# Taking all arithmetic off GpSimd in a two-layer hybrid decoder step

## The chip, the cores and the metric

One core of one Trainium2 chip runs the whole program. The metric is the device time of one execution in microseconds. Engines are TensorE (PE, with its weight loads as PEld), VectorE (DVE), ScalarE (ACT), GpSimd (POOL) and SyncE (SP), whose queue issues nearly all the DMAs.

## The reference

288 tokens (256 of one prompt and 8 samples of 4) pass through two layers. In each layer the normalised residual stream feeds one input projection whose columns go to three token mixers and three gates:

- gated DeltaNet: short convolution on q, k and v, then a chunked form with a triangular solve and a state S;
- retention: rotary q and k, fixed decay per head, a state R;
- mLSTM: exponential gates, a state C and a normaliser n.

```
R = R * c_dec + einsum(k_c * k_dec, v_c)               # retention
S = S * exp(g_last) + einsum(k_c * ..., v_new)         # DeltaNet
Cm = s_dec * Cm + einsum(kw, v_c)                      # mLSTM
x1 * cos - x2 * sin, x1 * sin + x2 * cos               # rotary
```

Each mixer's output is normalised, gated, projected, merged by the gates and projected out; then come a layer norm, a feed-forward part (1024 to 4096 to 1024, squared ReLU) and a layer norm. The updated states of prompt and samples are outputs too.

## The kernel before

Activations lie transposed: features on the 128 partitions, the 288 tokens along the free axis. A weight block (128x1024 fp32, 512 KB) is loaded by SP, split by ScalarE (`wh`, L358) and VectorE (`wl`, L360) into a high and a low part, and multiplied in three passes (`mm3`, L364): 24 matmuls of 288 columns for each 128 outputs. Inside the mixers these projection matmuls also serve as filling (L504) between the small dependent matmuls. Tile's scheduler sets the order on each engine by priority (order in the program) and readiness; at run time every engine takes its instructions in that order. SP too is in order, its DMAs included. Tiles of one kind share a pool: `B` (5040 bytes for each partition) has 18 buffers, and a tile waits for a free one.

In order of the program, for each layer:

- L586 `conv_group`, three times: GpSimd copies the sample's old rows (L591) and the new conv state (L600, L601); ScalarE and VectorE do the convolution.
- L622 to L762: gates, decays and cumulative sums in small VectorE operations on few rows; `dec` (L724) and the transposes behind it need them.
- L572 `rotary`, for rq and rk: two DMAs swap the halves into `rot`, VectorE multiplies by cos (L576), GpSimd by sin (L577), VectorE adds (L578).
- L764 to L797: keys are transposed and copied to KR (L768), squared and summed (`sumsq`, L412), and `rsqrt` (L379) runs eleven small VectorE operations. GpSimd later scales KR by the decay into KP (L858).
- L839 to L847: GpSimd scales the decay matrix E1 by beta (L839), VectorE multiplies it with the key products (L846) into MM. MM goes out to DRAM and returns by blocks (L862 to L867), 15 steps on VectorE invert the diagonal blocks (L869 to L874), the result returns as qc, and GpSimd spreads it into QL (L1056) and masks MM into E32 and E128 (L1062, L1064) for the solve.
- `qmask` (L880): GpSimd multiplies 32 sample columns of four heads with a 0/1 table into 128x1024, so that one matmul (`cross`, L893) picks a sample's rows. It is called for retention (L1017), DeltaNet (L1122, twice) and mLSTM (L1147).
- `vexp` (L925): two GpSimd multiplications with a 0/1 column (L929), three times a layer.
- `finish` (L957): sum of squares (L965), a chain of small VectorE operations (L967 to L974, with `rsqrt`), a scaling (L975), then transposes on PE (L982) and gating (L990, L992).
- `update` (L932): each of four groups of eight states of 128x128. For retention the decay is a constant and the evacuation of the product does all (L948). For DeltaNet and mLSTM GpSimd first multiplies the states by the decays (L937, 128x1024), then VectorE adds the product from PSUM in two halves (L952). The updates wait in a list, `later`, and `tick` runs one behind each tile of the next projection, the gate tiles `pg` of L1252 among them.

Of the kernel before, what the change touches and what calls it, by code (L numbers as in the profile page):

```python
# [58 lines left out]
for _n, _s in (("rm", T), ("mrst", T), ("sgn", 1), ("dsel", 64), ("kdec", 9), ("qdec", 1), ("stk", 10), ("ohbh", 32),  # L59
               ("gsel", 44),  # L60
               ("cos", T), ("sin", T), ("rdiag", 512), ("roff", 512), ("rsam", 128), ("ohr", 256), ("m32", 128),
               ("m128", 128), ("cm16", 128)):
    CONST[_n] = (_W, _s)
    _W += _s
# [3 lines left out]
def host_consts():  # L68
    c = np.zeros((P, CONST_W), np.float32)

    def put(n, a):
        o, s = CONST[n]
        c[:, o:o + s] = a
# [24 lines left out]
    put("rsam", np.where(le, np.exp((tt[None, :] - tt[:, None]) * lg[hh][:, None] * le), 0.0) * ks)  # L98
    put("ohr", np.broadcast_to((np.arange(NB)[:, None] == (np.arange(32) // NS)[None, :]).reshape(1, -1), (P, 256)))
    put("ohbh", ((bb[:, None] == np.arange(NB)[None, :])[:, :, None]  # L100
# [153 lines left out]
def tile_trunk(ctx, tc, a):  # L254
# [4 lines left out]
    def pool(name, bufs, **k):  # L259
        return ctx.enter_context(tc.tile_pool(name=name, bufs=bufs, **k))  # L260
# [3 lines left out]
    xp = pool("xp", 1)  # L264
    bp = pool("bp", 18)
    rp = pool("rp", 9)
# [41 lines left out]
    ones = cp.tile([P, P], F32, name="ones")  # L308
    V.memset(ones, 1.0 / 128.0)
    RB = cp.tile([P, T], F32R, name="RB")  # L310
    V.memset(RB.bitcast(F32), 0.0)
# [91 lines left out]
    def transpose9(src_p, src_s, evac):  # L403

        for g, (u0, u1) in enumerate(GRP):
# [4 lines left out]
            evac(u0, u1, ps[:, :(u1 - u0) * P].rearrange("p (u s) -> p u s", s=P))  # L410

    def sumsq(dst, src9):  # L412

        sq = u9(B("sq"))
        S.activation(sq, src9, AF.Square)
        V.tensor_reduce(dst, sq, axis=AX.X, op=ALU.add)

# [45 lines left out]
    for l in range(L):  # L463
# [108 lines left out]
        def rotary(X_):  # L572
            Y_ = h4(B("rot"))
            SP.dma_start(Y_[0:64], X_[64:128])
            SP.dma_start(Y_[64:128], X_[0:64])
            V.tensor_tensor(X_, X_, bcm(C("cos"), 4), op=ALU.mult)  # L576
            G.tensor_tensor(Y_, Y_, bcm(C("sin"), 4), op=ALU.mult)  # L577
            V.tensor_tensor(X_, X_, Y_, op=ALU.add)  # L578
            return X_
# [6 lines left out]
        def conv_group(gi, seg, st=None, done=()):  # L586
            CV = B("CV")
            cv = CV[:, :4 * CVW].rearrange("p (h w) -> p h w", w=CVW)
            cvs = cv[:, :, SB0:SB0 + 56].rearrange("p h (b w) -> p h b w", w=7)
            G.memset(cv[:, :, 0:3], 0.0)  # L590
            G.tensor_copy(cvs[:, :, :, 0:3],  # L591
                          cstate[:, 96 * gi:96 * gi + 96].rearrange("p (h b w) -> p h b w", h=4, b=NB))

            def ev(j, ps):
                S.copy(cv[:, j, 3:SB0], ps[:, :TP])
                S.copy(cvs[:, j, :, 3:7], ps[:, TP:T].rearrange("p (b t) -> p b t", t=NS))  # L596
            proj(seg, ev, st, done)

            ncv = K("ncv", 4, 27)
            G.tensor_copy(ncv[:, :, 0:3], cv[:, :, SB0 - 3:SB0])  # L600
            G.tensor_copy(ncv[:, :, 3:27].rearrange("p h (b w) -> p h b w", w=3), cvs[:, :, :, 4:7])  # L601
            G.dma_start(a["o_conv"][l, :, 108 * gi:108 * gi + 108], ncv.rearrange("p h w -> p (h w)"))
            CO = B("CO")
            co = CO[:, :4 * CVW].rearrange("p (h w) -> p h w", w=CVW)
            n = CVW - 3
            G.memset(co[:, :, n:CVW], 0.0)
            for j in range(4):
                S.activation(co[:, j, :n], cv[:, j, 0:n], AF.Copy, scale=VEC(l, "conv", gi * 4 + j))
                for w in range(1, 4):
# [156 lines left out]
        co, cs_ = conv["dk"]  # L766
        KR = u9(B("KR"))
        transpose9(lambda c, h: co[:, h, c * P:(c + 1) * P], cs_, lambda u0, u1, ps: S.copy(KR[:, u0:u1], ps))  # L768
        sumsq(ssqk[:, 1], KR)
        rqk = K("rqk", 2, 9)  # L770
# [67 lines left out]
        S.activation(E1[:, 8], ps, AF.Exp, bias=gcol[:, 8:9], scale=-1.0)  # L838
        G.tensor_tensor(E1, E1, bc(br2, P), op=ALU.mult)  # L839
        MM = E1  # L840
        for u0, u1 in GRP:
            ps = PX("G")
            for u in range(u0, u1):
                PE.matmul(ps[:, (u - u0) * P:(u - u0 + 1) * P], kt(u), kt(u), start=True, stop=True)
            fill(FILL_M[1])
            V.tensor_tensor(MM[:, u0:u1], E1[:, u0:u1], ps[:, :(u1 - u0) * P].rearrange("p (u s) -> p u s", s=P),  # L846
                            op=ALU.mult)  # L847

# [7 lines left out]
        PT = E2  # L856
        KP = KR
        G.tensor_tensor(KP, KR, bc(egl, P), op=ALU.mult)  # L858

# [19 lines left out]

        def qmask(qs_ap):  # L880
            m_ = B("qm")[:, :1024].rearrange("p (h b t) -> p h b t", h=H, b=NB)
            q4 = qs_ap.rearrange("p (h t) -> p h t", h=H)
            G.tensor_tensor(m_, q4.unsqueeze(2).to_broadcast([P, H, NB, 32]),
                            C("ohr").rearrange("p (b t) -> p b t", b=NB).unsqueeze(1).to_broadcast([P, H, NB, 32]),
                            op=ALU.mult)
            return m_
# [6 lines left out]
        def cross(ps, qm, st, q, w=P):  # L893
            for i in range(8):
                b, h = 2 * q + i // 4, i % 4
                PE.matmul(ps[32 * h:32 * h + 32, :w], qm[:, h, b, :], st[:, i, :],
                          start=b == 0, stop=b == NB - 1, tile_position=(0, 32 * h))
# [27 lines left out]
        def vexp(src, w):  # L925
            v_ = stack(src, 1, w).rearrange("p (h v) -> p h v", h=H)
            m_ = B("vx", F32R)[:, :1024].rearrange("p (h b v) -> p h b v", h=H, b=2)
            for b_ in range(2):
                G.tensor_scalar(m_[:, :, b_, :], v_.bitcast(F32), C("stk")[:, 4 + b_:5 + b_], None, op0=ALU.mult)  # L929
            return m_  # L930

        def update(st, q, kx, vx, dec, out):  # L932

            st = st[:, :, :P]
            pre = not isinstance(dec, list)
            if pre:
                G.tensor_tensor(st, st, bc(dec[:, 8 * q:8 * q + 8], P), op=ALU.mult)  # L937
            s4 = st.rearrange("p (b h) v -> p b h v", h=H)
            for hh in range(2):
# [6 lines left out]
                for h in (2 * hh, 2 * hh + 1):  # L946
                    if not pre:
                        V.scalar_tensor_tensor(s4[:, :, h, :], s4[:, :, h, :], dec[h], pv[:, :, h % 2, :],  # L948
                                               op0=ALU.mult, op1=ALU.add)
                if pre:  # L950
                    hs = s4[:, :, 2 * hh:2 * hh + 2, :]
                    V.tensor_tensor(hs, hs, pv, op=ALU.add)  # L952
            SP.dma_start(out[l, q].rearrange("p (i v) -> p i v", v=P), st)
# [62 lines left out]
        transpose9(lambda c, h: rv[:, h, c * P:(c + 1) * P], rvs, lambda u0, u1, ps: S.copy(RV[:, u0:u1], ps))  # L1016
        qm = qmask(rqs)  # L1017
        vx, kx = vexp(rvs, C("stk")[:, 6:10]), kexp(rks)
# [18 lines left out]
        for q in range(4):  # L1037
# [17 lines left out]
        QL = u9(B("QL"))  # L1055
        G.tensor_tensor(QL.rearrange("p u (k j) -> p u k j", j=16), qc.unsqueeze(2).to_broadcast([P, 9, 8, 16]),  # L1056
                        C("cm16").rearrange("p (k j) -> p k j", j=16).unsqueeze(1).to_broadcast([P, 9, 8, 16]),
# [3 lines left out]
        E32 = B("E32")[:, :1024].rearrange("p (u s) -> p u s", s=P)  # L1061
        G.tensor_tensor(E32, MM[:, :8], bcm(C("m32"), 8), op=ALU.mult)  # L1062
        E128 = MM
        G.tensor_tensor(E128[:, :8], MM[:, :8], bcm(C("m128"), 8), op=ALU.mult)  # L1064

# [55 lines left out]
        fin_dp = finish(OT, rqk[:, 0], zg, VEC(l, "dnn", 0), 0, 0, 8)  # L1121
        km, qm = qmask(cs_), qmask(cs_q)  # L1122
        kx = kexp(cs_)
# [22 lines left out]
        transpose9(lambda c, h: mv[:, h, c * P:(c + 1) * P], mvs, lambda u0, u1, ps: S.copy(MV[:, u0:u1, :P], ps))  # L1146
        qm_m = qmask(mqs)  # L1147
        vx_m, kx_m = vexp(mvs, WX[:, 1]), kexp(mks)
# [353 lines left out]
```

## Time and profile before

| | |
|---|---|
| median of 3 runs | 1285.8 us (1285.58 to 1287.79) |
| the profiled execution | 1285.11 us |
| its span, first to last instruction | 1283.3 us |
| busy: PE, PEld, DVE, ACT, POOL | 94%, 91%, 71%, 47%, 10% of the span |
| mean granted clock of TensorE | 0.971 |

The span holds both layers: the mixers of layer 0 run to about 285 us, its gates, output and feed-forward part to about 640 us, and layer 1 repeats this from there. The shares are means over these parts; what a wait costs is read in its own part.

### The profile page before, as it was taken

Reading aid. Unit: us, or ns where it says so; the run is one execution under the profiler, and the core shown is the slowest. Engines: PE = TensorE matmul, PEld = TensorE weight load, DVE = VectorE, ACT = ScalarE, POOL = GpSimd, SP = SyncE. Lnnn points to the kernel's source line nnn. Section 1 sums busy time; section 2 is a strip of 40 time slices with the busy share of each in tenths; the row PEclk is TensorE's granted clock in tenths of the full one; section 3 lists DMA queues with packets and bytes.
Section 4 is the critical chain, followed back from the end, with each engine's and each line's share of the span. In section 5 each row is a group of like instructions: output and inputs, shape, how many; then the busy total and the mean of one; then the engine's idle time right before and its main releaser. Section 6 shows DMA issues by size and latency. Waiting matters only on the chain.

```text
span 1283.3 us, 22945 instructions
## 1 busy us (share of the span) xinstructions
PE 1201.7 (94%) x9210; PEld 1169.4 (91%) x9210; DVE 909.0 (71%) x1617; ACT 597.1 (47%) x1006; POOL 126.6 (10%) x107
## 2 busy tenths in 40 slices
PE   9989899889999999999997988998899998999995
PEld 8978799789999899999996987997799998999995
DVE  6988846596558974566899877556856688645665
ACT  5645324433445653455584532453334566534532
POOL 1113400330000000000000413004200000000000
PEclk9989999889999999999998998998899998999998
DMA  8443624348554465555714454253575543655551
GB/s 311 124 146 107 214 85 152 124 181 243 166 167 123 142 181 164 168 168 162 245 57 133 119 176 154 90 182 140 169 211 164 165 156 94 193 166 165 164 165 38
DMA packets 69794, 201.27 MB, mean 157 GB/s; under 512 B 11688, under 2 KB 22232, under 8 KB 69560
## 3 DMA queue, kind: packets, MB, share of 16 engines
q1 hardware_dynamic: 68744, 197.64, 49.1%
q0 software_dynamic: 944, 2.17, 0.5%
q8 instruction: 72, 1.18, 0.4%
q14 instruction: 34, 0.28, 0.1%
HBM read 180.62 MB, written 17.03 MB: 154 GB/s over the span
## 4 chain that ended last, share of the span: by engine, by line
PE 71%; DVE 18%; DMA 4%; ACT 3%; issue 3%; SPq 1%; DVEq 0%; ACTq 0%
PE f L369 9%; PE f L367 9%; PE f L368 9%; PE pj L504 6%; DVE wl L360 5%; PE pg L367 4%; PE pg L368 4%; PE pg L369 4%; PE pj L369 2%; PE pj L368 2%; PE pj L367 2%; PE br L367 2%; PE br L368 2%; PE br L369 2%; DMA wr<-in_w_ff 1%
## 5 line engine op out<-in xcount | busy, mean ns | idle before, releaser
L360 DVE TENSOR_TENSOR wl<-wr,wh 128x1024 fp32r<-128x1024 f32 x292 | 370.8, 1272 | 182.2 <-ACT wh L358 175.3
L358 ACT CAST wh<-wr 128x1024 fp32r<-128x1024 f32 x292 | 306.2, 1050 | 398.6 <-PE f L368 96.0
L369 PE MATMUL f<-fh,wl 128*128 128x288 f32 x512 | 151.2, 295 | 0.0
L367 PE MATMUL f<-fh,wh 128*128 128x288 f32 x512 | 151.1, 295 | 0.0
L368 PE MATMUL f<-fl,wh 128*128 128x288 f32 x512 | 151.0, 295 | 0.0
L369 PE MATMUL f<-XH,wl 128*128 128x288 f32 x416 | 122.5, 295 | 1.3 <-DVE wl L360 1.3
L368 PE MATMUL f<-XL,wh 128*128 128x288 f32 x416 | 123.1, 296 | 0.0
L367 PE MATMUL f<-XH,wh 128*128 128x288 f32 x416 | 122.9, 296 | 0.0
L367 PE MATMUL pg<-XH,wh 128*128 128x288 f32 x384 | 116.6, 304 | 0.0
L368 PE MATMUL pg<-XL,wh 128*128 128x288 f32 x384 | 114.9, 299 | 0.0
L369 PE MATMUL pg<-XH,wl 128*128 128x288 f32 x384 | 114.3, 298 | 0.0
L369 PE MATMUL pj<-XH,wl 128*128 128x288 f32 x352 | 107.2, 306 | 6.6 <-DVE wl L360 6.6
L367 PE MATMUL pj<-XH,wh 128*128 128x288 f32 x352 | 106.9, 304 | 1.7 <-ACT CV L596 1.7
L368 PE MATMUL pj<-XL,wh 128*128 128x288 f32 x352 | 106.1, 302 | 0.0
L504 PE MATMUL pj<-XH,wh 128*128 128x288 f32 x320 | 99.9, 312 | 0.0
L504 PE MATMUL pj<-XL,wh 128*128 128x288 f32 x320 | 98.1, 306 | 0.0
L504 PE MATMUL pj<-XH,wl 128*128 128x288 f32 x320 | 97.8, 306 | 0.0
L369 PEld LDWEIGHTS f<-fh,wl 128*128 128x128 f32 x512 | 96.3, 188 | 0.1
L367 PEld LDWEIGHTS f<-fh,wh 128*128 128x128 f32 x512 | 96.2, 188 | 0.2
L368 PEld LDWEIGHTS f<-fl,wh 128*128 128x128 f32 x512 | 96.2, 188 | 0.1
L369 PEld LDWEIGHTS f<-XH,wl 128*128 128x128 f32 x416 | 78.4, 189 | 1.8 <-DVE wl L360 1.7
L367 PEld LDWEIGHTS f<-XH,wh 128*128 128x128 f32 x416 | 78.6, 189 | 0.0
(508 smaller groups left out, 2887.9 us busy)
## 6 DMA issues: line engine op xcount, KB each, us to landing
wr<-in_w_in SPq DMA_DIRECT2D x141, 512.0 KB
wr<-in_w_ff SPq DMA_DIRECT2D x128, 512.0 KB
wr<-in_w_out SPq DMA_DIRECT2D x16, 512.0 KB
S<-in_state_ml_C SPq DMA_DIRECT2D x8, 516.0 KB
S<-in_state_ret_R SPq DMA_DIRECT2D x8, 512.0 KB
out_s_R<-S SPq DMA_DIRECT2D x8, 512.0 KB
S<-in_state_dn_S SPq DMA_DIRECT2D x8, 512.0 KB
out_s_S<-S SPq DMA_DIRECT2D x8, 512.0 KB
```

The source lines that it names most:

```text
L358: S.copy(hi[:, k, :], r[:, k, :])
L360: V.tensor_tensor(lo[:, k, :], r[:, k, :], hi[:, k, :].bitcast(F32), op=ALU.subtract)
L367: PE.matmul(ps, hi[:, k, :], xh[k], start=start and k == 0, stop=False)
L368: PE.matmul(ps, hi[:, k, :], xl[k], start=False, stop=False)
L369: PE.matmul(ps, lo[:, k, :], xh[k], start=False, stop=stop and k == KT - 1)
L504: ins = PE.matmul(self.ps[:, :T], self.w[i // 2][:, k, :], (xh, xl, xh)[i][k], start=self.k == 0, stop=self.k == 23)
```

## The change

Nothing but memsets and DMA issues stays on GpSimd.

- `update` drops L937; eight VectorE operations of 128x128 (state times decay plus product from PSUM) take the place of the two additions.
- `qmask` becomes one VectorE copy of 128 columns into one of two standing tiles, QM, which were set to zero once. The call for mLSTM moves behind the DeltaNet's state products, since it reuses the first of the two. The table `ohr` goes.
- The sin half of `rotary`, QL, E32 and E128 move to VectorE; the masks of `vexp` and the conv copies to ScalarE.
- Beta is multiplied in while MM is evacuated: nine operations of 128x128 in place of three of up to 512 columns.
- KP is written from the transposes' PSUM by VectorE, and ScalarE squares from PSUM; KR and `sumsq` go.
- Pool `B` has 16 buffers for 18, which makes room for QM.

```diff
-    bp = pool("bp", 18)
+    bp = pool("bp", 16)
...
+    QM = [cp.tile([P, H, T], F32, name=f"QM{i}") for i in range(2)]
+    for m_ in QM:
+        G.memset(m_, 0.0)
...
-            G.tensor_tensor(Y_, Y_, bcm(C("sin"), 4), op=ALU.mult)
+            V.tensor_tensor(Y_, Y_, bcm(C("sin"), 4), op=ALU.mult)
...
-            G.tensor_copy(cvs[:, :, :, 0:3],
-                          cstate[:, 96 * gi:96 * gi + 96].rearrange("p (h b w) -> p h b w", h=4, b=NB))
+            S.copy(cvs[:, :, :, 0:3],
+                   cstate[:, 96 * gi:96 * gi + 96].rearrange("p (h b w) -> p h b w", h=4, b=NB))
...
-            G.tensor_copy(ncv[:, :, 0:3], cv[:, :, SB0 - 3:SB0])
-            G.tensor_copy(ncv[:, :, 3:27].rearrange("p h (b w) -> p h b w", w=3), cvs[:, :, :, 4:7])
+            S.copy(ncv[:, :, 0:3], cv[:, :, SB0 - 3:SB0])
+            S.copy(ncv[:, :, 3:27].rearrange("p h (b w) -> p h b w", w=3), cvs[:, :, :, 4:7])
...
-        KR = u9(B("KR"))
-        transpose9(lambda c, h: co[:, h, c * P:(c + 1) * P], cs_, lambda u0, u1, ps: S.copy(KR[:, u0:u1], ps))
-        sumsq(ssqk[:, 1], KR)
+        KP, KS = u9(B("KP")), u9(B("KS"))
+
+        def ev_k(u0, u1, ps):
+            S.activation(KS[:, u0:u1], ps, AF.Square)
+            if u0 < 8:
+                V.tensor_tensor(KP[:, u0:u1], ps, bc(egl[:, u0:u1], P), op=ALU.mult)
+        transpose9(lambda c, h: co[:, h, c * P:(c + 1) * P], cs_, ev_k)
+        V.tensor_reduce(ssqk[:, 1], KS, axis=AX.X, op=ALU.add)
...
-        G.tensor_tensor(E1, E1, bc(br2, P), op=ALU.mult)
...
-            V.tensor_tensor(MM[:, u0:u1], E1[:, u0:u1], ps[:, :(u1 - u0) * P].rearrange("p (u s) -> p u s", s=P),
-                            op=ALU.mult)
+            for u in range(u0, u1):
+                V.scalar_tensor_tensor(MM[:, u], E1[:, u], br2[:, u:u + 1], ps[:, (u - u0) * P:(u - u0 + 1) * P],
+                                       op0=ALU.mult, op1=ALU.mult)
...
-        KP = KR
-        G.tensor_tensor(KP, KR, bc(egl, P), op=ALU.mult)
...
+            m_ = QM[i]
+            V.tensor_copy(m_.rearrange("p h (b w) -> p h b w", w=36)[:, :, :, 0:NS],
+                          qs_ap.rearrange("p (h b t) -> p h b t", h=H, b=NB))
...
-                PE.matmul(ps[32 * h:32 * h + 32, :w], qm[:, h, b, :], st[:, i, :],
+                PE.matmul(ps[32 * h:32 * h + 32, :w], qm[:, h, 32 * b:32 * b + 32], st[:, i, :],
...
-                G.tensor_scalar(m_[:, :, b_, :], v_.bitcast(F32), C("stk")[:, 4 + b_:5 + b_], None, op0=ALU.mult)
+                S.activation(m_[:, :, b_, :], v_.bitcast(F32), AF.Copy, scale=C("stk")[:, 4 + b_:5 + b_])
...
-            if pre:
-                G.tensor_tensor(st, st, bc(dec[:, 8 * q:8 * q + 8], P), op=ALU.mult)
...
-                if pre:
-                    hs = s4[:, :, 2 * hh:2 * hh + 2, :]
-                    V.tensor_tensor(hs, hs, pv, op=ALU.add)
+                        continue
+                    for b in range(2):
+                        i = 8 * q + 4 * b + h
+                        V.scalar_tensor_tensor(s4[:, b, h, :], s4[:, b, h, :], dec[:, i:i + 1], pv[:, b, h % 2, :],
+                                               op0=ALU.mult, op1=ALU.add)
```

QL (L1056), E32 (L1062) and E128 (L1064) change only from `G.` to `V.`, and `qm_m = qmask(mqs, 0)` moves from L1147 to just ahead of L1233.

## Rows read from the trace of the kernel before

**Rows 1.** The page, its first part: busy us and share of the span of each engine, and its instructions.

```profile
PE 1201.7 (94%) x9210; PEld 1169.4 (91%) x9210; DVE 909.0 (71%) x1617; ACT 597.1 (47%) x1006; POOL 126.6 (10%) x107
```

**Rows 2.** The waits of PE: engine, tile and line that waited, what ended the wait; total us, times, longest us. The two layers are added up.

```profile
PE tp L982 <- DVE OR L975: 11.4, 2, 5.8
PE Xs L1213 <- DVE R L1196: 10.0, 2, 5.0
PE dec L724 <- DVE dr L720: 7.9, 2, 4.8
PE up L943 <- DVE S L952: 4.9, 2, 2.5
PE stk L908 <- ACT sx L904: 3.2, 2, 2.0
PE tp L409 <- DVE cd L778: 3.0, 2, 1.5
PE tp L982 <- DVE OM L975: 2.0, 2, 1.1
```

**Rows 3.** Seven stretches just behind a wait of PE: us from:to and length, busy us and instructions of PE, PEld, DVE, ACT and POOL, granted clock of TensorE (1.00 is 2.4 GHz), DMA share, GB/s.

```profile
76.60:82.10 5.50, 5.50 (x24) 5.50 (x25) 4.17 (x9) 1.34 (x2) 0.00 (x0) 0.50 0.38 112
161.30:164.00 2.70, 2.69 (x13) 2.69 (x14) 2.70 (x6) 0.00 (x0) 0.00 (x0) 0.50 0.83 249
252.10:256.20 4.10, 4.09 (x17) 4.10 (x18) 0.00 (x0) 0.27 (x1) 0.00 (x0) 0.50 0.42 128
279.20:283.50 4.30, 4.30 (x19) 4.30 (x20) 4.27 (x14) 1.65 (x4) 0.00 (x0) 0.50 0.52 205
790.40:795.50 5.10, 5.10 (x23) 5.10 (x24) 3.65 (x11) 0.59 (x1) 0.00 (x0) 0.50 0.68 209
882.40:887.70 5.30, 5.30 (x23) 5.30 (x24) 0.24 (x1) 1.18 (x2) 0.00 (x0) 0.50 0.32 102
909.90:915.00 5.10, 5.10 (x23) 5.10 (x24) 5.07 (x16) 1.65 (x4) 0.00 (x0) 0.50 0.65 212
```

**Rows 4.** The order of time of GpSimd and of VectorE in layer 0: start us, us, what, shape, count [idle before]. GpSimd first, then VectorE.

```profile
242.69 7.45 POOL L937 TENSOR_TENSOR S<-S,DEC 128x1024 f32<-128x1024 f32 x4
...
266.69 7.59 POOL L937 TENSOR_TENSOR S<-S,DEC 128x1024 f32<-128x1024 f32 x4 [1.19 <-PE mcr L896]
...
73.24 2.22 POOL L577 TENSOR_TENSOR rot<-rot,cst 128x1152 f32<-128x1152 f32 x1 [1.32 <-DMA rot<-rq]
...
244.95 6.28 DVE L360 TENSOR_TENSOR wl<-wr,wh 128x1024 fp32r<-128x1024 f32 x1 [3.17 <-PE pj L369]
...
266.81 1.80 DVE L967 TENSOR_TENSOR fss<-fss,dn 128x8 f32<-128x8 f32 x1
...
272.48 1.82 DVE L382 TENSOR_SCALAR rsy<-fss 128x8 int32<-128x8 int32 x1
...
147.70 1.85 DVE L382 TENSOR_SCALAR rsy<-fss 128x8 int32<-128x8 int32 x1
...
151.55 1.92 DVE L384 TENSOR_TENSOR rst<-rsy 128x8 f32<-128x8 f32 x1
```

**Rows 5.** VectorE by form: line, operation, out<-in, shape, count | busy us, mean ns of one | its idle time before and what ended it. L360 comes first, blocked ones among it; the others are prices of operations that nothing blocked.

```profile
L360 DVE TENSOR_TENSOR wl<-wr,wh 128x1024 fp32r<-128x1024 f32 x292 | 370.8, 1272 | 182.2 <-ACT wh L358 175.3 <-PE pj L369 6.3
L386 DVE TENSOR_SCALAR rst<-rst 128x8 f32<-128x8 f32 x6 | 1.0, 167 | 0.1
L576 DVE TENSOR_TENSOR rq<-rq,cst 128x1152 f32<-128x1152 f32 x2 | 2.7, 1354 | 0.4 <-DMA rot<-rq 0.4
L975 DVE TENSOR_TENSOR OM<-OM,fr 128x1024 f32<-128x1024 f32 x2 | 2.4, 1216 | 0.0
L1116 DVE SCALAR_TENSOR_TENSOR S<-S,egl,S 128x128 f32<-128x128 f32 x8 | 2.2, 340 | 0.0
L952 DVE TENSOR_TENSOR S<-S,up 128x512 f32<-128x512 f32 x32 | 21.9, 684 | 12.1 <-issue 10.2 <-PE up L943 1.9
L569 DVE COPY cs<-rq 128x128 f32<-128x128 f32 x2 | 0.5, 227 | 0.1
```

**Rows 6.** ScalarE by form: as group 5.

```profile
L918 ACT ACTIVATE sb<-sb,cst 128x512 f32<-128x512 f32 x6 | 4.3, 721 | 0.1
L615 ACT COPY csd<-CO 128x128 f32<-128x128 f32 x6 | 1.9, 310 | 2.3 <-DVE CO L613 2.3
```

**Rows 7.** Two stretches as in group 3: the finish of retention ahead of the transposes of L982, and the stretch of the state updates, both in layer 0.

```profile
143.10:161.20 18.10, 12.44 (x111) 11.08 (x109) 17.58 (x40) 5.61 (x10) 10.27 (x5) 0.98 0.51 173
262.00:308.00 46.00, 42.64 (x328) 38.64 (x327) 39.36 (x82) 15.35 (x24) 10.83 (x6) 0.93 0.65 221
```

**Rows 8.** The order of time of VectorE in layer 0 around the key matrix.

```profile
101.58 2.19 DVE L392 TENSOR_TENSOR rsu<-rsu,rst 128x9 f32<-128x9 f32 x1
103.78 3.25 DVE L578 TENSOR_TENSOR rk<-rk,rot 128x1152 f32<-128x1152 f32 x1
106.96 1.97 DVE L393 SCALAR_TENSOR_TENSOR rqk<-rsu,rsy 128x9 f32<-128x9 f32 x1
```

**Rows 9.** The chain that ended last, in order of time: start us, us, what.

```profile
73.38 2.39 DVE RB L706
75.78 0.45 DVE RB L706
127.78 4.57 DMA S<-in_state_ret_R
```

More of the change, by code (lines that the diff above doesn't have):

```diff
@@ L60 @@
                ("gsel", 44),
-               ("cos", T), ("sin", T), ("rdiag", 512), ("roff", 512), ("rsam", 128), ("ohr", 256), ("m32", 128),
+               ("cos", T), ("sin", T), ("rdiag", 512), ("roff", 512), ("rsam", 128), ("m32", 128),
                ("m128", 128), ("cm16", 128)):
@@ L98, in host_consts @@
     put("rsam", np.where(le, np.exp((tt[None, :] - tt[:, None]) * lg[hh][:, None] * le), 0.0) * ks)
-    put("ohr", np.broadcast_to((np.arange(NB)[:, None] == (np.arange(32) // NS)[None, :]).reshape(1, -1), (P, 256)))
     put("ohbh", ((bb[:, None] == np.arange(NB)[None, :])[:, :, None]
@@ L410, in transpose9 @@
             evac(u0, u1, ps[:, :(u1 - u0) * P].rearrange("p (u s) -> p u s", s=P))
[L412 to L416, printed above, removed]
     ps = PX("warm")
@@ L878, in tile_trunk, with qmask @@
         SP.dma_start(qc, qd.rearrange("b i u j -> (b i) u j"))
[L880 to L885, printed above, removed]
+        def qmask(qs_ap, i):
+            m_ = QM[i]
+            V.tensor_copy(m_.rearrange("p h (b w) -> p h b w", w=36)[:, :, :, 0:NS],
+                          qs_ap.rearrange("p (h b t) -> p h b t", h=H, b=NB))
             return m_
@@ L1016, in tile_trunk @@
         transpose9(lambda c, h: rv[:, h, c * P:(c + 1) * P], rvs, lambda u0, u1, ps: S.copy(RV[:, u0:u1], ps))
-        qm = qmask(rqs)
+        qm = qmask(rqs, 0)
         vx, kx = vexp(rvs, C("stk")[:, 6:10]), kexp(rks)
@@ L1055, in tile_trunk @@
         QL = u9(B("QL"))
-        G.tensor_tensor(QL.rearrange("p u (k j) -> p u k j", j=16), qc.unsqueeze(2).to_broadcast([P, 9, 8, 16]),
+        V.tensor_tensor(QL.rearrange("p u (k j) -> p u k j", j=16), qc.unsqueeze(2).to_broadcast([P, 9, 8, 16]),
                         C("cm16").rearrange("p (k j) -> p k j", j=16).unsqueeze(1).to_broadcast([P, 9, 8, 16]),
@@ L1061, in tile_trunk @@
         E32 = B("E32")[:, :1024].rearrange("p (u s) -> p u s", s=P)
-        G.tensor_tensor(E32, MM[:, :8], bcm(C("m32"), 8), op=ALU.mult)
+        V.tensor_tensor(E32, MM[:, :8], bcm(C("m32"), 8), op=ALU.mult)
         E128 = MM
-        G.tensor_tensor(E128[:, :8], MM[:, :8], bcm(C("m128"), 8), op=ALU.mult)
+        V.tensor_tensor(E128[:, :8], MM[:, :8], bcm(C("m128"), 8), op=ALU.mult)
         Wt = E32
@@ L1121, in tile_trunk @@
         fin_dp = finish(OT, rqk[:, 0], zg, VEC(l, "dnn", 0), 0, 0, 8)
-        km, qm = qmask(cs_), qmask(cs_q)
+        km, qm = qmask(cs_, 0), qmask(cs_q, 1)
         kx = kexp(cs_)
@@ L1146, in tile_trunk @@
         transpose9(lambda c, h: mv[:, h, c * P:(c + 1) * P], mvs, lambda u0, u1, ps: S.copy(MV[:, u0:u1, :P], ps))
-        qm_m = qmask(mqs)
         vx_m, kx_m = vexp(mvs, WX[:, 1]), kexp(mks)
@@ L1232, in tile_trunk @@
             later.append(lambda q=q: update(sts[q], q, kx, vx, DEC[:, 0], a["s_S"]))
+        qm_m = qmask(mqs, 0)
         ps = PX("mcr")
```

## The prediction

> **What bounds the kernel now.** I began with the busy shares [rows 1]: PE is busy 94% of the span, VectorE 71%, GpSimd 10%. GpSimd is no bound by its own work. The question is where PE, the engine that bounds, stands still, and whether GpSimd is behind it. The waits of PE [rows 2] answer the first half: the largest are in the mixers, each once in a layer, and each ends on a VectorE operation: 11.4 us in all on the finish of retention (OR L975), 10.0 us on the DeltaNet sample correction (R L1196), 7.9 us on `dr`, 4.9 us on the first state update, 2.0 us on the finish of mLSTM (OM L975).
>
> Then I read the granted clock behind those waits [rows 3]. In all seven stretches PE is busy without a break, but at 0.50, which is 1.2 of 2.4 GHz, for 2.7 to 5.5 us. Work done there takes twice its time, so half of each stretch belongs to the price of the wait ahead of it.
>
> Third, why VectorE is late, from the order of time [rows 4]. `wl` L360 takes 6.28 us at 244.95 us, where its mean is 1.27 [rows 5]; it ends 1.1 us after a run of four state multiplications on GpSimd (242.69 us, 7.45 us long). On 8 columns, L967 to L382 (four operations from 266.81 to 272.48 us) take 1.80 us in the first and 1.82 in the last, beside the second such run; L382 to L384 (three from 147.70 us) 1.85 and 1.92. The same kind of operation takes 0.167 us where GpSimd rests [rows 5]. So VectorE is held up until a GpSimd operation ends, and these operations lie on the chains that PE waits for. This is what the change can give back: not GpSimd's 126.6 us, but VectorE's blocked time where PE waits for it.
>
> **The change part by part.** The sum is made against the profiled execution, 1285.1 us, a span of 1283.3 with 1.8 around it. The median of the runs is 0.7 above, which I add at the end.
>
> *State decays in the evacuation, the place ahead of Xs.* With L937 gone `wl` takes its mean: 5.0 us less in layer 0. Of the 5.0 us that PE waits in each layer I leave 0.2. The slow stretches behind (252.1 and 882.4 us, 4.1 and 5.3 us at half clock) cost 2.05 and 2.65; they go with the wait. Sum: 2 x 4.8 + 4.7 = **14.3 us less**.
>
> *The same edit, the updates.* The four blocked operations from 266.81 us give back 4 x 1.65 = 6.6 us in a layer, ahead of both OM and the first evacuation. PE's waits there are 4.9 + 2.0 us, the slow stretches behind (279.2 and 909.9 us) cost 2.15 + 2.55: 11.6 in all. Against that, an update now takes eight operations at 0.340 (the nearest form: 128x128, one input in PSUM) in place of two at 0.684 [rows 5]: 2.72 - 1.37 = 1.35 more, 10.8 a layer. In the stretch of the updates VectorE is busy 39.4 of 46 us [rows 7]; 39.4 - 6.6 + 10.8 = 43.6, and the stretch itself would shrink by 5.8 to 40. By full prices VectorE has 3.6 us too much; if back-to-back operations overlap, and since part can run on under the branch matmuls behind, nothing. I take the middle, 1.8 a layer: 11.6 - 3.6 = **8 us less** (bounds 4.4 and 11.6).
>
> *The finish of retention.* Here VectorE is full: 17.58 busy of 18.1 us in layer 0 [rows 7], and PE's wait is as long in layer 1. Three blocked operations give back 3 x 1.73 = 5.2. What lands on VectorE: QL, a 128x1152 operation at 1.354; E32 and E128, 128x1024 at 1.216 each; two `qmask` copies of 128 columns at 0.227 [rows 5]: 4.2 if all of it falls here. The masks need MM alone and may run earlier, where VectorE has holes; then it is 1.8. Net 1.0 to 3.4 a layer; middle 2.2. The wait stays at 3.5 of 5.7, so most of the slow clock behind it (1.35 and 2.55 lost) stays too; I give it 1. Sum: **5.4 us less** (bounds 2.0 and, with all the clock, 10.7). What is late next is the same chain, then W behind it.
>
> *Rotary.* In layer 0 `RB` L706 takes 2.39 us [rows 9] beside the sin product on GpSimd (73.24 us, 2.22 long [rows 4]); its twin right behind takes 0.45. That is 1.94 of the 4.8 us wait of `dec`; I take 1 of the 2.75 lost in the slow stretch at 76.6 us. **2.9 us less** (bounds 1.9 and 4.7). The sin product costs VectorE 1.354, placed beside the cos product after `dec`, under filling matmuls. In layer 1 nothing collides there; its 3.1 us stay. The two swap DMAs were awaited by the cos product already, so no new wait is queued on VectorE.
>
> *Beta and the key matrix.* VectorE loses 2.0, 1.9 and 1.8 us to GpSimd from 101.58 us on [rows 8], where about 0.17, 1.36 and 0.17 are needed. It gains 1.354 for rk's sin product and 9 x 0.340 - (2 x 0.684 + 0.3) = 1.4 for the nine evacuations: some 3 us earlier for MM, and with it its DMA to DRAM and back, the inversion, and the copies behind which `stk` L908 waits 3.2 us in both layers. **2 us less** (bounds 0 and 3.2).
>
> *KP and the squares.* Two evacuations at 0.684 more on VectorE in a layer, one long square less on ScalarE, a collision less: 1.5 us of PE's wait for L409 in a layer could go or double. I take 0 (bounds 3 either way).
>
> *ScalarE.* 18 conv copies at no more than 0.310 and 12 masks of `vexp` at 0.721 [rows 6]: 5.6 + 8.7 = 14.3 us, on an engine busy 47%. They lie under projection matmuls; in order behind each mask stand weight casts, which run a tile ahead. Without that cover all 14.3 would count. In layer 0 the first copies wait for a DMA on an engine that feeds PE. **1 us more** (bounds 0 and 14).
>
> *Sixteen buffers.* Two less in `B`, against one to three `qm` tiles not taken. By my count of the mLSTM loads 17 tiles want 16 places, where 18 had 18: a state load waits for a temporary to go. SP issues in order, so weight loads queue behind it. **1 us more** (nearest row: one state load, 4.57 us [rows 9]; bounds 0 and two of these, 9). A gain is not counted, since no row shows a load that waits for a `qm` tile.
>
> Sum: -14.3 - 8 - 5.4 - 2.9 - 2 + 1 + 1 = -30.6; 1285.1 - 30.6 + 0.7 = **1255 us**. With all the gains at their far bounds and no cost it is 1285.8 - 47.5 = 1238.
>
> **Rivals.**
>
> *VectorE becomes the bound.* 10.8 us a layer in the updates and 4.2 in the finish come just where it is full. For it: the 17.58 of 18.1 and 43.6 of 40 above. Against it: blocked time counts as busy. If both places give nothing, 13.4 of the 30.6 are lost: 1285.8 - 17.2 = 1268.6 us. The Trainium skill (Perfetto Trace Analysis, Optimizing Scalar/DVE Operations) speaks for this one: with a saturated VectorE, work may be better off on ScalarE or even GpSimd. It adds that their shared port may spoil that; the 1.85 us operations show the spoiling.
>
> *Only one operation's worth of blocking.* If a VectorE operation waited only for the GpSimd operation under way, `wl` would lose at most 1.9 us, and the rest of its 5.0 would have another cause that stays. The step ahead of Xs would give 2 x 1.9 with no clock: 3.8 for 14.3, and 1285.8 - 20.1 = 1265.7 us. Against it: its end follows that of the whole run. The Trainium skill (SBUF — State Buffer, Who interferes with whom) words the lock so: whoever starts first holds the port pair for the whole instruction and the other waits. By that, `wl` should have got in at the next boundary; the trace has it wait through the run.
>
> *Slower: state loads wait for buffers.* Place: the loads of four state tiles in three mixers of two layers. A load that finds no free buffer waits until an update's tile is out and then for itself: 2 x 4.57 = 9.1 us, and 2.3 for a slow clock behind it as in group 3: 11.4. From the third such place on it eats the 30.6; with four the time is 1285.8 - 30.6 + 45.6 = 1300.8 us. Against it: DeltaNet and mLSTM free as many `qm` tiles as places are lost.
>
> *The change gives nothing,* because VectorE's long operations are not GpSimd's doing: 1285.8 us. Only the coincidence of ends stands against it, but at every place that I read.
>
> **How the numbers follow.** Forecast 0.63; VectorE bound 0.20; one operation's blocking 0.07; buffers 0.07; nothing 0.03. The first three are faster by over 0.2% (2.6 us, about what a measurement of this kernel can tell from no change): 0.90; same 0.03; slower 0.07. The range runs from 1239, by the far gains, over both milder rivals to 1272, where some of ScalarE's or the buffers' price has come on top; outside lie the buffers as a rival, the case of nothing and some tail.
>
> **What would show it.** In the new profile: no GpSimd arithmetic; no 128x8 VectorE operation above 0.3 us; the wait of Xs near zero and no half clock behind it; waits for OR of about 3.5 us; the updates as eight operations of about 0.34 with PE hardly waiting at L943; some shorter wait at `dec` in layer 0 alone. I am wrong if the Xs wait stays, if PE waits for `wl` among the gate tiles, or if `cross` waits for state loads.

## The result, and the profile after

The changed kernel takes 1244.5 us (median of 4 runs, 1242.2 to 1249.4) where the kernel before, beside it, takes 1286.8. The ratio is 0.9676, with a 95% interval of 0.9643 to 0.9708. Measured once more with the last experiments it was 1240.7 us, 0.9644 (0.9607 to 0.9682). The gain is 42 to 46 us; 31 were forecast. Two measurements of one kernel differ by 4 us here, so smaller differences between experiments are read from their traces.

The profiled execution after took 1243.5 us, with a span of 1241.7. Its busy time by engine, to be held against [rows 1]:

```profile
PE 1192.0 (96%) x9210; PEld 1160.6 (93%) x9210; DVE 881.6 (71%) x1747; ACT 603.6 (49%) x1034; POOL 14.0 (1%) x41
```

VectorE has 130 instructions more and is busy 27 us less. The span less PE's busy time, which is what PE stood still, falls from 81.6 to 49.7 us; PE's busy time falls by 9.7 us: ahead of the end of the program, 50.0 us of it lay in stretches of half clock, 31.6 do now, and half of that difference is 9.2. Together 41.6 us. Which waits went is seen in the waits of PE after, against [rows 2]:

```profile
PE tp L981 <- DVE OR L974: 6.0, 2, 3.0
PE f L377 <- ACT XH L1360: 5.9, 2, 3.7
PE dec L720 <- DVE dr L716: 4.6, 2, 2.4
PE pj L371 <- DVE wl L362: 3.4, 3, 2.1
PE br L369 <- ACT tg L1256: 1.8, 2, 0.9
...
PE stk L907 <- ACT sx L903: 1.4, 1, 1.4
...
PE pg L371 <- DVE wl L362: 1.1, 2, 0.6
```

Xs, the first evacuation of the updates and OM are gone; OR and `dec` have lost 5.4 and 3.3 us; `br` and `pg` are new, 2.9 us. The same table before had 6.6 us for the wait of projection tiles on `wl`, of which 5.1 were one wait in layer 1 (from 678.2 us); it has 3.4 now.

Next come stretches of time after (columns as in group 3): one behind Xs, four at half clock, and the two that answer to [rows 7].

```profile
239.00:252.00 13.00, 13.00 (x110) 12.38 (x109) 10.51 (x34) 9.38 (x15) 0.00 (x0) 1.00 0.54 177
...
152.60:156.00 3.40, 3.40 (x17) 3.40 (x16) 3.40 (x7) 0.59 (x1) 0.00 (x0) 0.50 0.46 149
...
272.00:275.40 3.40, 3.40 (x16) 3.40 (x16) 3.40 (x11) 0.00 (x0) 0.00 (x0) 0.50 0.84 251
688.50:695.30 6.80, 6.17 (x28) 6.14 (x29) 5.25 (x20) 1.61 (x4) 0.00 (x0) 0.50 0.26 73
879.60:883.00 3.40, 3.14 (x13) 3.14 (x14) 3.40 (x11) 0.00 (x0) 0.00 (x0) 0.50 0.91 292
...
133.60:151.70 18.10, 15.22 (x131) 13.69 (x129) 16.21 (x43) 6.72 (x11) 0.00 (x0) 1.00 0.60 209
249.00:288.00 39.00, 37.67 (x296) 33.44 (x294) 35.14 (x119) 13.39 (x21) 0.00 (x0) 0.96 0.71 234
```

Behind Xs the clock stays at 2.4 GHz. A shorter stretch at 1.2 GHz remains behind the finish of retention, and one of 3.4 us has come behind each new `pg` wait.

Last, VectorE's order of time after: at Xs, in the finish of retention, and ahead of the first `pg` wait (PE starts again at 271.45 us):

```profile
238.38 0.28 DVE L1194 TENSOR_TENSOR R<-R,smp 128x128 f32<-128x128 f32 x1
...
241.46 1.22 DVE L362 TENSOR_TENSOR wl<-wr,wh 128x1024 fp32r<-128x1024 f32 x1 [0.20 <-ACT wh L360]
...
147.49 1.22 DVE L1061 TENSOR_TENSOR E<-E,cst 128x1024 f32<-128x1024 f32 x1
148.62 0.16 DVE L395 SCALAR_TENSOR_TENSOR fr<-rsu,rsy 128x8 f32<-128x8 f32 x1
...
148.77 1.22 DVE L1063 TENSOR_TENSOR E<-E,cst 128x1024 f32<-128x1024 f32 x1
149.90 0.16 DVE L973 TENSOR_SCALAR fr<-fr 128x8 f32<-128x8 f32 x1
...
150.54 1.22 DVE L974 TENSOR_TENSOR OR<-OR,fr 128x1024 f32<-128x1024 f32 x1
...
268.38 1.89 DVE L950 SCALAR_TENSOR_TENSOR S<-S,DEC,up 128x128 f32<-128x128 f32 x7
270.19 1.21 DVE L362 TENSOR_TENSOR wl<-wr,wh 128x1024 fp32r<-128x1024 f32 x1
```

`wl` takes 1.22 us, where it took 6.28. The elementwise operations on 8 columns (`rsqrt` and the like) take 0.16 to 0.17 us on the mean. E32 and E128 (L1061, L1063) stand between the steps of OR's chain, each step of 0.16 us behind one mask of 1.22. The split that PE awaits among the gate tiles stands right behind seven update operations.

### The profile page after: what moved, and what is told of

It reads as the page before. It is cut to its first block, busy times and chain, and to the rows that moved or that the text cites. A ratio compares the mean times of both kernels' runs of the same rounds, so it can differ in the third digit from the quotient of the medians.

```text
span 1241.7 us, 22988 instructions
## 1 busy us (share of the span) xinstructions
PE 1192.0 (96%) x9210; PEld 1160.6 (93%) x9210; DVE 881.6 (71%) x1747; ACT 603.6 (49%) x1034; POOL 14.0 (1%) x41
## 4 chain that ended last, share of the span: by engine, by line
PE 79%; DVE 12%; DMA 3%; ACT 3%; issue 2%; SPq 0%; ACTq 0%; DVEq 0%
PE f L371 10%; PE f L369 10%; PE f L370 10%; PE pj L500 6%; PE pg L371 4%; PE pg L369 4%; PE pg L370 4%; PE pj L371 3%; PE pj L370 3%; PE pj L369 3%; DVE wl L362 2%; PE br L369 2%; PE br L371 2%; PE br L370 2%; DVE CO L606 1%
## 5 line engine op out<-in xcount | busy, mean ns | idle before, releaser
L360 ACT CAST wh<-wr 128x1024 fp32r<-128x1024 f32 x292 | 306.0, 1049 | 382.5 <-PE f L370 98.9
L362 DVE TENSOR_TENSOR wl<-wr,wh 128x1024 fp32r<-128x1024 f32 x292 | 356.2, 1223 | 182.7 <-ACT wh L360 182.3
L371 PE MATMUL pj<-XH,wl 128*128 128x288 f32 x352 | 105.1, 300 | 3.4 <-DVE wl L362 3.4
L369 PE MATMUL pj<-XH,wh 128*128 128x288 f32 x352 | 105.9, 301 | 1.7 <-ACT CV L592 1.7
L370 PE MATMUL pj<-XL,wh 128*128 128x288 f32 x352 | 104.9, 298 | 0.0
L500 PE MATMUL pj<-XH,wh 128*128 128x288 f32 x320 | 98.3, 307 | 0.0
L500 PE MATMUL pj<-XH,wl 128*128 128x288 f32 x320 | 97.0, 303 | 0.3 <-DVE wl L362 0.3
L500 PE MATMUL pj<-XL,wh 128*128 128x288 f32 x320 | 96.7, 302 | 0.0
```

Of the source, the lines that this page charges most:

```text
L360: S.copy(hi[:, k, :], r[:, k, :])
L362: V.tensor_tensor(lo[:, k, :], r[:, k, :], hi[:, k, :].bitcast(F32), op=ALU.subtract)
L369: PE.matmul(ps, hi[:, k, :], xh[k], start=start and k == 0, stop=False)
L370: PE.matmul(ps, hi[:, k, :], xl[k], start=False, stop=False)
L371: PE.matmul(ps, lo[:, k, :], xh[k], start=False, stop=stop and k == KT - 1)
L500: ins = PE.matmul(self.ps[:, :T], self.w[i // 2][:, k, :], (xh, xl, xh)[i][k], start=self.k == 0, stop=self.k == 23)
```

## The experiments

The theory: a GpSimd operation holds VectorE up, through a whole run of such operations, and the time came from the places where PE waits for VectorE. The rivals: it holds it for one operation at most; the waits were waits for data; the order of VectorE's list decides.

**The update alone, on the kernel before.**

```diff
-                G.tensor_tensor(st, st, bc(dec[:, 8 * q:8 * q + 8], P), op=ALU.mult)
...
-                    V.tensor_tensor(hs, hs, pv, op=ALU.add)
...
+                        V.scalar_tensor_tensor(s4[:, b, h, :], s4[:, b, h, :], dec[:, i:i + 1], pv[:, b, h % 2, :],
+                                               op0=ALU.mult, op1=ALU.add)
```

> The kernel before with the update's decays alone moved into the evacuation. Theory (GpSimd's four multiplications in a row hold VectorE until the last ends): the waits for R and at the first evacuation go, by the prediction's first two terms 22.3 us less than before, about 1263.5 (1260 to 1267). Rival, one operation's worth of blocking: 3.8 + 8 less, about 1274. Rival, VectorE bound in the updates: 14.3 less, about 1271.5. Rival, no blocking: 1286, since VectorE has 10.8 us a layer more.

Measured: 1262.7 us, 0.9799 (0.9776 to 0.9823), 25.7 us less. The waits for R, S and OM are gone from its table. In the stretch of its updates:

```profile
250.00:296.00 46.00, 46.00 (x368) 41.47 (x368) 41.55 (x144) 18.54 (x30) 3.21 (x2) 1.00 0.67 230
```

PE is busy for all 46 us at full clock; VectorE, with 41.55, is not the bound. The two forecast terms were 22.3; this edit is over half of the whole gain.

**E32, E128 and QL alone, on the kernel before.** `G.` to `V.` in three lines.

> The kernel before with QL, E32 and E128 alone moved to VectorE; every other engine keeps its order. Theory: VectorE gains three blocked operations of 1.73 us and takes 3.8 us of work, the wait for OR falls from 11.4 us to 7 to 10 in all (vexp and the query mask still stand on GpSimd), 2 to 7 us less: about 1281. Rival, VectorE is full there: the wait for OR stays or grows, 0 to 4 us more, 1286 to 1290.

Measured: 1285.6 us, 0.9979 (0.9958 to 1.0001), 2.7 us less, of which the interval leaves 0 to 5. The wait for OR:

```profile
PE tp L982 <- DVE OR L975: 8.1, 2, 4.1
```

It fell from 11.4 to 8.1: three more operations on VectorE, and PE waits less for OR.

**The multiplication back on GpSimd, in the changed kernel.** The reverse of the first diff.

> The changed kernel with the state multiplication back on GpSimd and two additions on VectorE. Theory: the wait for R or for wl comes back, 18 to 26 us more than the changed kernel: about 1266. Rival, the gain in this place comes from the other edits around it (masks, buffers): less than 6 us more, under 1250.

Measured: 1259.1 us, 0.9776 (0.9739 to 0.9814): 13 to 17 us more than the changed kernel, less than the theory has. The waits, and VectorE's order of time at Xs and at the updates:

```profile
PE tp L981 <- DVE OM L974: 8.5, 2, 4.2
PE Xs L1211 <- DVE R L1194: 6.3, 2, 3.2
```

```profile
238.32 1.78 DVE L883 COPY QM<-cs 128x128 f32<-128x128 f32 x1
240.02 2.00 DVE L1194 TENSOR_TENSOR R<-R,smp 128x128 f32<-128x128 f32 x1
...
260.80 1.86 DVE L387 TENSOR_TENSOR rst<-rst,fss 128x8 f32<-128x8 f32 x1
...
263.18 1.34 DVE L388 TENSOR_SCALAR rst<-rst 128x8 f32<-128x8 f32 x1
```

Four multiplications in a row stand beside each of these (233.65 us on; 257.6 to 266.3). Here every VectorE operation loses one operation's worth at most, and gets in at the next boundary: the rival's rule. But ahead of R two such operations stand in a row in VectorE's list, which lose 3.3 us together; the chain of OM has several.

**Four idle multiplications.** Nobody waits for them; the order of every other engine is the same.

```diff
...
+        for q in range(4):
+            G.tensor_tensor(SCR.rearrange("p (i v) -> p i v", v=120), cst[:, o_:o_ + 960].rearrange("p (i v) -> p i v", v=120),
+                            bc(t2[:, 8 * q:8 * q + 8], 120), op=ALU.mult)
```

> The changed kernel plus four GpSimd multiplications in a row in each layer, right behind the cross products of DeltaNet's states: they read constants (128x960) and eight columns of the scaled sample product and write a scratch that nobody reads. Nothing waits for them, and no other engine's order changes. Theory: a VectorE operation in that stretch lasts until the end of the run, over 4 us, PE waits 3 to 5 us in each layer and loses 1 to 2 more to the clock: 8 to 13 us more, about 1255. Rival, one operation's worth: no VectorE operation loses more than 2.0 us, 0 to 4 us more. Rival, the old wait was one of data: nothing, 1244.5.

Measured: 1247.9 us, 0.9686 (0.9652 to 0.9719): 1 to 5 us more by the ratios, whose intervals overlap with those of the changed kernel. GpSimd runs from 240.92 us for 8.23 us; VectorE beside it:

```profile
243.51 2.14 DVE L363 TENSOR_TENSOR wl<-wr,wh 128x1024 fp32r<-128x1024 f32 x1 [0.21 <-ACT wh L361]
245.57 1.89 DVE L1206 TENSOR_SCALAR mgate<-mgate,vec 128x288 f32<-128x288 f32 x1
```

So the collision needs no data in common. Each of these operations lost one operation's worth at most, and the four GpSimd operations took 8.23 us where four of 1.79 and their gaps make 7.4: VectorE held GpSimd up as well. The theory's whole run fell here.

**The disputed cost by itself.** Behind the end of the changed kernel, 32 runs of four GpSimd operations, with one VectorE operation in each that a chain of small ScalarE copies starts at one of four delays.

```diff
+            for x_ in BS:
+                G.tensor_tensor(r8(x_), r8(x_), bc(bd, P), op=ALU.mult)
...
+            for _ in range(n):
+                S.copy(bq, bt)
+            last = t_()
...
```

> The changed kernel with a measurement behind its end: 32 times four GpSimd operations of 128x1024 in a row, and one VectorE operation that starts at one of four delays into the run. GpSimd: four multiplications in place in four tiles (as L937 of before), four into one tile (as in the run with the four idle ones), four memsets. VectorE: the weight split wl, a product of two SBUF inputs, a product on 8 columns, a scalar operation on 288, one with an input in PSUM, a sum over 1024. Theory, through the whole run: against four tiles wl lasts up to the end of the fourth, 5 to 7 us; against one tile, where the operations had gaps of 0.08 us, one operation's worth, 2 to 3. Rival, one operation's worth always: no VectorE operation above its own time plus 1.95 us. Memsets, which read nothing: nobody waits.

Measured: GpSimd's operations take 1.89 us alone. VectorE's order of time, the first delay of each kind (0.2 to 0.5 us into GpSimd's first operation):

```profile
1243.83 2.47 DVE L1516 TENSOR_TENSOR bL<-bW,bH 128x1024 fp32r<-128x1024 f32 x1 [2.02 <-ACT bH L1515]
...
1280.66 2.76 DVE L1520 TENSOR_TENSOR bV<-bW,bq 128x1024 f32<-128x1024 f32 x1 [4.65 <-ACT bq L1550]
...
1317.72 1.70 DVE L1524 TENSOR_TENSOR bV<-bq 128x8 f32<-128x8 f32 x1 [4.65 <-ACT bq L1550]
...
1350.85 1.84 DVE L1528 TENSOR_SCALAR bV<-bW,bq 128x288 f32<-128x288 f32 x1 [4.73 <-ACT bq L1550]
...
1384.24 0.35 DVE L1532 SCALAR_TENSOR_TENSOR bV<-bW,bq,bps 128x128 f32<-128x128 f32 x1 [4.65 <-ACT bq L1550]
...
1417.59 1.22 DVE L1537 TENSOR_REDUCE bV<-bW 128x8 f32<-128x1024 f32 x1 [6.11 <-ACT bW L1536]
...
1488.15 1.22 DVE L1516 TENSOR_TENSOR bL<-bW,bH 128x1024 fp32r<-128x1024 f32 x1 [5.05 <-ACT bH L1515]
```

The first four wait for the end of GpSimd's first operation; the next two delays give shorter waits, and the longest, which falls into the second operation, gives a wait for the end of that one. An operation with one input in PSUM (L1532) and a sum (L1537) never wait, at any of four delays; nor does `wl` beside memsets (last line). Four tiles or one make no difference. The Trainium skill (SBUF — State Buffer, Who interferes with whom) says that VectorE with two SBUF inputs collides with a GpSimd instruction that reads SBUF but not with one that only writes, that one-input operations outside the two-port modes and sums do not, and that whoever issues first keeps the shared pair for the whole instruction. All rows of this run agree (in which mode L1528 ran, no row shows).

**Forty moments.** As before, `wl` alone, at 40 delays from 0.1 to 4.3 us into the run.

> The changed kernel with a measurement behind its end: 40 times four GpSimd multiplications in place in four tiles, and one weight split wl that starts at one of 40 delays, some 0.1 us apart, in the first two of the four. Rival that one operation's worth is a rule: wl never lasts longer than 1.2 plus 1.95 us. Theory that the 6.28 us of before depends on the moment: at some delays, near 0.41 us into an operation, wl lasts to the end of the fourth, 5 to 8 us.

Measured, over all 40 (ns, shortest, median and longest):

```profile
L1507 DVE TENSOR_TENSOR bL<-bW,bH x40: 1225/2083/2856, 1244.9 to 1593.9; 128x1024 fp32r<-128x1024 f32 x40
```

Never more than one operation's worth, at 0.42 us into the second operation too (2.56 us); `wl` of before, 0.41 us into the second, lasted 6.28.

**The masks moved out of retention's finish, in the changed kernel.** E32 and E128 stand behind the inversion.

```diff
         SP.dma_start(qc, qd.rearrange("b i u j -> (b i) u j"))
...
+        V.tensor_tensor(E32, MM[:, :8], bcm(C("m32"), 8), op=ALU.mult)
...
+        V.tensor_tensor(E128[:, :8], MM[:, :8], bcm(C("m128"), 8), op=ALU.mult)
```

> The changed kernel with E32 and E128 moved in the program to the place behind the inversion, so that VectorE does them in its idle time at about 130 us and not between the steps of retention's finish. Theory (VectorE is full in the finish and nothing else makes it late): the wait for OR falls from 6.0 us to 1 to 2, with the half clock behind it 4 to 8 us less than the changed kernel, 1237 to 1241. Rival, the chain of OR waits for something else there: within 1 us. Rival, the masks delay the next step (weights, updates) in the new place: 0 to 4 us more.

Measured: 1243.0 us, 0.9683 (0.9657 to 0.9709): no change. VectorE's order of time in layer 0:

```profile
150.18 1.22 DVE L362 TENSOR_TENSOR wl<-wr,wh 128x1024 fp32r<-128x1024 f32 x1
151.31 0.16 DVE L395 SCALAR_TENSOR_TENSOR fr<-rsu,rsy 128x8 f32<-128x8 f32 x1
...
151.46 1.22 DVE L362 TENSOR_TENSOR wl<-wr,wh 128x1024 fp32r<-128x1024 f32 x1
152.59 0.16 DVE L977 TENSOR_SCALAR fr<-fr 128x8 f32<-128x8 f32 x1
```

Two weight splits took the two masks' places, and PE waits 3.0 us for OR as it did (2.2 in layer 1, for 3.0). So the edit took no load off the chain: in the 18.1 us up to OR's first transpose VectorE is busy 16.18 us, and 16.21 in the changed kernel. Its list has a long operation behind each step, and where two left, the scheduler put in two others that were ready. Whether that load makes OR late is not settled here; the last experiment bears on it.

**The sin products back on GpSimd, in the changed kernel.** One line in `rotary`.

> The changed kernel with the sin product of both rotary steps back on GpSimd. Theory: RB is held up again in layer 0, the wait for dec goes from 4.6 to about 7 us, and rk comes 2 us later: 2 to 6 us more than the changed kernel, about 1248. Rival, the product on VectorE costs as much as the blocking did: within 1.5 us.

Measured: 1248.4 us, 0.9717 (0.9698 to 0.9736), 5 to 9 us more. The wait for `dec`, and what was held up in each layer:

```profile
PE dec L720 <- DVE dr L716: 9.6, 2, 5.1
```

```profile
74.30 2.92 DVE L702 TENSOR_TENSOR RB<-rc,RB 4x288 fp32r<-4x288 f32 x2
...
689.63 2.40 DVE L713 TENSOR_TENSOR drv<-vec,M 4x8 f32<-4x8 f32 x1
```

The wait is 5.0 us longer: two operations on four rows, one in each layer, lost 2.0 and 2.2 us.

**The masks of vexp back on GpSimd, in the changed kernel.** One line.

> The changed kernel with the masks of vexp back on GpSimd. Theory: three pairs of 1.78 us in a layer block VectorE, one of them beside the inversion or the finish of retention: 2 to 8 us more, about 1249. Rival, ScalarE's 8 us for them stood on a chain: 1 to 5 us less than the changed kernel.

Measured: 1240.0 us, 0.9649 (0.9624 to 0.9674), not to be told from the changed kernel. In its trace the wait of `pg` and the half clock behind it are gone, and the twelve masks (1.84 us each) cost VectorE 0.3 to 0.4 us at four short operations of the inversion. Two `wl` lost 0.2 us each. Neither side was right: these GpSimd operations meet little that PE waits for, and what the masks cost on ScalarE is no more than the 4 us by which two measurements of the changed kernel differ.

**Query masks and beta back on GpSimd, in the changed kernel,** with 18 buffers.

```diff
+        G.tensor_tensor(E1, E1, bc(br2, P), op=ALU.mult)
...
-            V.tensor_copy(m_.rearrange("p h (b w) -> p h b w", w=36)[:, :, :, 0:NS],
+            G.tensor_tensor(m_, q4.unsqueeze(2).to_broadcast([P, H, NB, 32]),
...
```

> The changed kernel with the query masks back as GpSimd multiplications with the 0/1 table into pool tiles (18 buffers, no standing tiles) and beta back as a GpSimd multiplication of E1. Theory: the masks of 2 to 3 us hold up single steps in the finish of retention (the wait for OR goes from 6.0 to 8 to 11 us in all, with half clock behind it) and beta makes the key matrix 2 us later: 6 to 12 us more than the changed kernel, about 1253, which is what the other runs left unaccounted for. Rival, these edits were worth nothing by themselves: within 2 us.

Measured: 1255.8 us against 1240.7 beside it, 15 us more; ratios 0.9753 (0.9714 to 0.9793) and 0.9644. Its waits:

```profile
PE tp L981 <- DVE OR L974: 4.7, 1, 4.7
PE tp L981 <- DVE rst L386: 4.6, 1, 4.6
PE Xs L1211 <- DVE R L1194: 3.1, 2, 1.6
...
PE KQs L853 <- DVE E L845: 2.1, 1, 2.1
```

Ten GpSimd operations are enough to bring 3.3 us at OR, 3.1 at Xs and 2.1 at the key matrix, while the waits for `dec` and of `pj` for `wl` fell by 2.0 and 2.1. Between the profiled executions PE stands still 10.8 us more (60.3 for 49.5) and is busy 7.3 us longer (1196.8 for 1189.5). The three edits that cost something when undone come to 33 to 41 us (the update 13 to 17, rotary 5 to 9, these 15) of 42 to 46; KP, the conv copies, QL, E32 and E128 were not undone by themselves. Such prices depend on the kernel around them: the update gave 25.7 us in the kernel before.

**The changed kernel again, and a version with more fill.**

> The changed kernel itself again, as the measure for the runs on this chip: 1244 (1241 to 1248).

It took 1240.7 us. The half clock that the first profile has at 152.6 us is absent here, with the same wait of 3.0 us ahead of it; so is the one behind the first `pg` wait in the run with the masks moved, where that wait is 0.6 us too. That part of a wait's price comes and goes.

The version has the masks of `vexp` on GpSimd, as in the run with them back, and more filling asked for ahead of `dec` and of OR:

```diff
-FILL_C = (3, 3, 2, 3)
+FILL_C = (11, 3, 2, 3)
...
-FILL_Q = (72, 8, 8, 2)
+FILL_Q = (96, 8, 8, 2)
...
-                S.activation(m_[:, :, b_, :], v_.bitcast(F32), AF.Copy, scale=C("stk")[:, 4 + b_:5 + b_])
+                G.tensor_scalar(m_[:, :, b_, :], v_.bitcast(F32), C("stk")[:, 4 + b_:5 + b_], None, op0=ALU.mult)
```

> The changed kernel with the masks of vexp on GpSimd (as in the run with them back), and with more filling matmuls, taken from later ones, ahead of two waits: 24 more ahead of the finish of retention (FILL_Q 72 to 96) and 24 more ahead of dec (FILL_C 3 to 11 steps of three). If these waits (6.0 and 4.6 us in the changed kernel) are chains of fixed length, the fill covers 2 to 3 us at each of the four places: with the 3 us of the masks 8 to 12 us less than the changed kernel, about 1234. Rival, the fill is missed later (rotary's key, the solve): 0 to 4 us less.

Measured: 1237.8 us (1235.1 to 1238.6), 0.9608 (0.9568 to 0.9648), 3 us under the changed kernel beside it (1239.7 to 1245.5); the intervals of the ratios overlap. The wait for OR is gone from its table in both layers. VectorE's order of time in layer 0 shows why:

```profile
143.91 1.22 DVE L974 TENSOR_TENSOR OR<-OR,fr 128x1024 f32<-128x1024 f32 x1
...
146.11 1.35 DVE L1055 TENSOR_TENSOR QL<-qc,cst 128x1152 f32<-128x1152 f32 x1
...
151.43 1.22 DVE L1061 TENSOR_TENSOR E<-E,cst 128x1024 f32<-128x1024 f32 x1
```

QL, its transpose and both masks, some 5.2 us, now stand behind OR, where they stood ahead of it. OR starts 22.2 us behind PE's first matmul of L1029, where it took 29.2 in the changed kernel. The filling itself did little of this: 149 projection matmuls stand between L1029 and OR's first transpose, where 142 stood, and 22 more have come between the seventh and the eighth transpose. So it was the new list that let OR move up: these four operations are 5.2 of the 7.0 us. VectorE's load ahead of OR had made it late. Why more filling gave this list is not shown.

The wait for `dec` is 5.1 us: the scheduler put none of the added matmuls ahead of `dec` (41 filling matmuls stand there in layer 0 in either version). In layer 1 PE waits 1.5 us at the key transposes (704.20 us), with a new stretch at half clock behind it:

```profile
704.40:714.60 10.20, 10.20 (x48) 9.85 (x47) 5.22 (x21) 6.13 (x22) 0.00 (x0) 0.50 0.15 48
```

## Why the prediction was right, and where it was not

The direction, and the reading that GpSimd's price is VectorE's held-up time where PE waits for it, held: of the seven waits in [rows 2], three went and four became shorter. The time, 1244.5, lies 10.5 us below the forecast and inside the range. Term by term:

- *The place ahead of Xs, 14.3, and the updates, 8.* Measured together by the first experiment: 25.7. The charge of 3.6 for VectorE's eight operations in place of two was not due in that run. They take about the price forecast (0.343 us for 0.340), but VectorE is busy 41.55 us in 46, and PE never waits there. In the changed kernel a small part of it came, with the gate tiles (below).
- *The mechanism behind Xs* was wrong as a rule. "Held up through the run" is true of one operation, `wl` at 244.95 us and its like in layer 1; everywhere else, and in the 60 trials by itself of operations that collide, it is one operation's worth at most. The rival that I gave 0.07 has the rule, and still not the time: the 5.0 us did go with L937. Why that `wl` lost three boundaries is open. It did so again at 6.28 us in both layers of the run with only the masks moved, ended 1.09 us after GpSimd's last operation each time, and no chosen moment brought it back.
- *The finish of retention, 5.4.* The wait fell by just that, 11.4 to 6.0. PE's work at half clock behind it, 7.8 us in [rows 3], is 3.4 now; half of that is loss, so 2.2 less where I gave 1. The reason holds: VectorE's long operations ahead of OR make it late, and the version whose list has four of them behind OR has no wait. What I had not seen is that the list decides which they are, so that moving two masks out changed nothing.
- *Rotary, 2.9.* Undoing it brought 5.0 us of wait. I counted layer 0 alone; in the changed kernel's list a second chain operation (`drv`) would stand beside GpSimd in layer 1. Against [rows 2] the wait itself fell by 3.3, 2.4 in layer 0 and 0.9 in layer 1, whose 3.1 I had left as they were.
- *Beta and the key matrix, 2; KP, 0.* The waits of `stk` fell by 1.8 and those of the key transposes (L409) by 2.1, 3.0 to 0.9. With beta and the query masks undone together, 15 us; I had not priced the query masks apart from the finish, and they also reach R.
- *ScalarE, 1.* PE waiting for `wl` among the gate tiles was one of my signs of being wrong, and it came: 1.1 us and half of twice 3.4 at half clock, some 4.5. The split stands right behind seven update operations, so it is VectorE's price that was charged to the updates. The wait is absent with the updates alone on the kernel before, with the update undone, and with the masks of `vexp` back on GpSimd, so it takes both edits; why VectorE's list then has this order is not shown. The time of the run without those masks on ScalarE does not confirm the size.
- *Sixteen buffers, 1.* No `cross` waits for a state load in the table after; before, `rcr` did, 1.5 us, and in the second profile of the changed kernel it does for 0.5.
- *Not named at all:* the wait on `wl` in layer 1, 5.1 to 2.1 us. VectorE's list has the split that was awaited ahead of a reciprocal of 1.95 us now (L651, 662.00 us), where it stood behind it (L655, 677.33 us); the 2.1 us are the wait for the next split. It stays 5.1 in both experiments on the kernel before and is 2.1 in the versions with conv copies on ScalarE, or 1.1 with query masks and beta back; the conv copies alone were not tried.

Of the rivals, VectorE as the bound, with nothing won in the updates and the finish, is refuted by the first experiment and the wait for OR; buffers by the waits after; and the case of nothing by the time.

## What to carry to other kernels

Price an engine that is not the bound by what its operations do to a neighbour that they hold up: look for short operations of that neighbour with ten times their usual duration, and ask whether a chain that the bounding engine awaits runs through them. A chain of short operations pays one whole operation of the other engine at each collision, so one long run beside a chain is dear and twelve operations beside little that is awaited cost nothing that could be measured (ratios of 0.9649 with them and 0.9644 without). When an engine's order is a list made beforehand, taking work off a chain helps only if the list lets the chain move up: moving two masks out brought two splits in, and a list with QL and the masks behind OR did what that edit did not. Read the order that came out, not the order that was asked for.

## What the hardware showed that was not expected

The holding up is mutual. VectorE's long two-input operations hold GpSimd as well: in the run of four, the operation behind the boundary at which `wl` got in took 2.87 us for 1.89. The run of four as a whole, beside a VectorE operation that waits, beside one with an input in PSUM, and beside `wl` against memsets, in GpSimd's order of time of the measurement behind the end:

```profile
1280.45 8.43 POOL L1502 TENSOR_TENSOR bS<-bS,bd 128x1024 f32<-128x1024 f32 x4 [0.83 <-ACT bq L1550]
...
1384.02 7.45 POOL L1502 TENSOR_TENSOR bS<-bS,bd 128x1024 f32<-128x1024 f32 x4 [0.83 <-ACT bq L1550]
...
1487.63 3.62 POOL L1512 MEMSET bS<- 128x1024 f32 x4 [0.80 <-ACT bS L1510]
```

The 0.98 us between the first two is most of the 1.22 us that such an operation takes by itself. The evacuations that the change puts in GpSimd's place have an input in PSUM: they are of the one kind of two-input operation that did not collide in any trial.
